# A decoder layer whose feed-forward products are taken by 2x2 blocks with seven multiplications

## The chip, the cores and the metric

The kernel runs on one core of a Trainium2 chip. The metric is the device time of one execution in microseconds (us). The engines are called as in the profile: PE (TensorE, matrix products; PEld is its loading of weights), DVE (VectorE), ACT (ScalarE), POOL (GpSimd) and SP (SyncE), which issues every DMA here.

## The reference

One layer of a hybrid decoder. It takes 1024 prompt tokens and 8 sample tokens (1032 columns in all), 1024 channels, and a feed-forward width of 2816. The part up to the mixing (projections, attention, pooling, gates) is the same in both kernels. The part that is changed computes, per token:

```
m  = sigmoid(gate_a) * (o @ w_attn_o) + sigmoid(gate_b) * B
x  = x + gt1 * (m @ w_out)
h2 = rmsnorm(x) * (1 + sc2) + sh2
gg, up = split(h2 @ w_gu)                    # w_gu: 1024 x (2 x 2816)
y  = x + gt2 * ((silu(gg) * up) @ w_down)    # w_down: 2816 x 1024
```

The sample tokens have shifts, scales and gates of their own; the prompt tokens share one set. All data is float32.

## The kernel before

Activations lie with channels on the 128 partitions and tokens along the free axis, in tiles of 128 channels. A float32 product is made of three matmuls in a 4-byte format of lower precision (`_mm3`, lines 70 to 73): each operand is split into a high part (a rounding copy on ACT, line 97) and a low part (source minus high part, on DVE or POOL, line 106), and high x high, high x low and low x high are summed in PSUM. So every operand costs one pass of ACT and one of DVE or POOL before PE may read it.

Tokens are worked on in three chunks of 344 columns (`C3`). The function `back` (line 1005) begins while attention is still running: it multiplies the attention output of the first six heads by `w_attn_o` for all chunks (tile `pm`, line 1066), then, chunk by chunk, adds the last two heads (`rest`, line 1038), multiplies by `w_out` (line 1099), adds the residual (line 999), forms the mean square with a product by ones (lines 1085, 1086), its root and reciprocal (lines 1113, 1114), and from these h2, split into `h2h` and `h2l`. The 8 weight tiles of `w_out` are split once and stay in SBUF for the three chunks.

`feed_forward` (line 1130) goes through the 22 tiles of the feed-forward width in four parts (`FPARTS`, 6, 6, 5 and 5 tiles). For each tile it loads and splits one weight tile of the gate half and one of the up half (`wload`, 128 x 1024 each), and for each chunk makes the two products over 8 tiles of channels (48 matmuls), then silu on ACT, the product on DVE and a split into `acth` and `actl`, which stay in SBUF. At the end of a part the products with `w_down` for the 8 tiles of output channels are added to x (line 999), which also stays in SBUF. The weights have four pairs of slots, so loading and splitting run ahead of PE.

The order is made by a planner. The program text is traced; the planner then simulates the engines and puts, on each engine, the instruction that is ready and stands first in the text, and sets the semaphores. Two of its rules matter for the steps below. First, tiles with one tag share its slots (`bufs` of them) in the order of the text: the next tile gets a slot when the tile that had it has been read for the last time, even if the data for the next one have long been there. Second, a pool that is opened over the memory or the PSUM banks of a closed pool is not written until everything in the closed pool is done. Each engine then runs its list in order.

## Time and profile before

| | us |
|---|---|
| median of 3 runs (1799.04 to 1801.34) | 1800.38 |
| span of the profiled execution | 1798.7 |
| PE busy | 1741.1 (97%) |
| DVE / ACT / POOL busy | 828.8 / 614.2 / 307.2 |

The own time of the profiled execution outside its span is not given apart; the median of the runs stands 1.7 us above the span, which is taken for what lies around it. PE busy means that a matmul is somewhere in the engine; matmuls overlap, so the distance from one start to the next says how fast PE works, not the duration of one. The stages follow one another: projections and the sample tokens with the gates as filler up to about 600 us, attention of the prompt up to 925 us, `w_out` up to 1047 us, feed-forward up to the end.

### The profile page before, as it was taken

How to read it: one execution, taken by the hardware profiler on the slowest of the kernel's cores; microseconds unless marked ns; L12 is line 12 of the kernel's file. 1: busy time of each engine (PE TensorE's matmuls, PEld its weight loads, DVE VectorE, ACT ScalarE, POOL GpSimd, SP SyncE). 2: the span in 40 equal slices, each digit the busy share in tenths (PEclk: the TensorE clock that was granted, in tenths of full speed). 3: DMA queues.
4: the chain of work that ended last, by engine and by line, in shares of the span. 5: the costliest groups of instructions: out<-in, count | busy, mean ns of one | idle time of the engine just before them, and what ended most of it. 6: DMA issues, size and time to landing. Idle time of an engine off the chain costs nothing.

```text
span 1798.7 us, 30723 instructions
## 1 busy us (share of the span) xinstructions
PE 1741.1 (97%) x11840; PEld 1641.8 (91%) x11840; DVE 828.8 (46%) x1731; ACT 614.2 (34%) x1521; POOL 307.2 (17%) x336
## 2 busy tenths in 40 slices
PE   6799999999999999999989999999999999999999
PEld 5799999789687899998889899999999999999999
DVE  5656665547332455555787852233222322242223
ACT  5433555546341355545542332211221112111210
POOL 2524201001011223222575630000000000000000
PEclk9899999999999999999999999999999999999999
DMA  9213635445636433335523211111111121111112
GB/s 376 63 58 105 209 99 151 147 131 158 186 101 204 157 124 125 124 122 179 158 86 97 70 42 53 36 48 60 47 42 36 53 59 39 30 62 47 39 57 82
DMA packets 112147, 182.70 MB, mean 102 GB/s; under 512 B 15193, under 2 KB 86770, under 8 KB 110978
## 3 DMA queue, kind: packets, MB, share of 16 engines
q1 hardware_dynamic: 112002, 180.75, 32.4%
q8 instruction: 93, 1.52, 0.4%
q14 instruction: 52, 0.43, 0.1%
HBM read 151.77 MB, written 28.93 MB: 100 GB/s over the span
## 4 chain that ended last, share of the span: by engine, by line
PE 80%; DMA 4%; DVE 4%; issue 2%; ACT 1%; POOL 1%; SPq 1%; DVEq 0%; ACTq 0%; POOLq 0%
PE pj L71 19%; PE pj L72 19%; PE pj L73 19%; PE kn L71 4%; PE kn L72 3%; PE kn L73 3%; PE dacc L958 2%; PE tpp L679 2%; PE ada_ps L142 1%; PE av L693 1%; PE av L694 1%; PE sc L71 1%; PE sc L73 1%; PE sc L72 1%; PE tp L628 1%
## 5 line engine op out<-in xcount | busy, mean ns | idle before, releaser
L73 PE MATMUL pj<-h2h,fw 128*128 128x344 f32 x1056 | 337.1, 319 | 0.0
L72 PE MATMUL pj<-h2l,fw 128*128 128x344 f32 x1056 | 336.9, 319 | 0.0
L71 PE MATMUL pj<-h2h,fw 128*128 128x344 f32 x1056 | 335.7, 319 | 0.0
L73 PEld LDWEIGHTS pj<-h2h,fw 128*128 128x128 f32 x1056 | 198.3, 188 | 0.0
L72 PEld LDWEIGHTS pj<-h2l,fw 128*128 128x128 f32 x1056 | 198.2, 188 | 0.0
L71 PEld LDWEIGHTS pj<-h2h,fw 128*128 128x128 f32 x1056 | 198.1, 188 | 0.0
L97 ACT ACTIVATE fw<-fraw 128x1024 fp32r<-128x1024 f32 (+2 forms) x76 | 72.0, 948 | 302.4 <-PE pj L72 302.4
L73 PE MATMUL pj<-acth,fw 128*128 128x344 f32 x528 | 169.0, 320 | 0.0
L72 PE MATMUL pj<-actl,fw 128*128 128x344 f32 x528 | 168.9, 320 | 0.0
L71 PE MATMUL pj<-acth,fw 128*128 128x344 f32 x528 | 168.6, 319 | 0.0
L71 PE MATMUL pj<-hh,wt_hi 128*128 128x344 f32 x480 | 159.8, 333 | 0.0
L1167 DVE TENSOR_TENSOR silu<-silu,pj 128x344 f32<-128x344 f32 x66 | 33.8, 512 | 270.7 <-PE pj L73 270.7
L72 PE MATMUL pj<-hl,wt_hi 128*128 128x344 f32 x480 | 157.5, 328 | 0.0
L73 PE MATMUL pj<-hh,wt_lo 128*128 128x344 f32 x480 | 157.4, 328 | 0.0
L71 PE MATMUL kn<-wuh,lh 128*128 128x256 f32 (+1 forms) x512 | 150.4, 294 | 1.9 <-ACT nr L903 1.0
L72 PE MATMUL kn<-wul,lh 128*128 128x256 f32 (+1 forms) x512 | 145.3, 284 | 0.0
L73 PE MATMUL kn<-wuh,ll 128*128 128x256 f32 (+1 forms) x512 | 144.9, 284 | 0.0
L902 ACT ACTIVATE dsq<-kn 128x256 f32<-128x256 f32 x256 | 95.1, 380 | 111.5 <-PE kn L73 103.5
L999 DVE SCALAR_TENSOR_TENSOR x<-pj,mod,x 128x344 f32<-128x344 f32 (+1 forms) x96 | 55.0, 573 | 149.9 <-PE pj L73 149.9
L106 DVE TENSOR_TENSOR fw<-fraw,fw 128x1024 fp32r<-128x1024 f32 (+2 forms) x76 | 83.5, 1099 | 76.5 <-ACT fw L97 74.5
L904 DVE TENSOR_REDUCE ssq<-dsq 128x8 f32<-128x512 f32 x128 | 86.7, 679 | 52.5 <-ACT dsq L902 52.0
L71 PEld LDWEIGHTS kn<-wuh,lh 128*128 128x128 f32 x512 | 96.6, 189 | 13.0 <-issue 5.7
(328 smaller groups left out, 3778.9 us busy)
## 6 DMA issues: line engine op xcount, KB each, us to landing
fraw<-wgu_t SPq DMA_DIRECT2D x44, 512.0 KB, 3.6
pg<-cpack SPq DMA_DIRECT2D x128, 144.0 KB, 2.4
ln<-cnat SPq DMA_DIRECT2D x128, 128.5 KB, 2.4
wraw<-wada_t SPq DMA_DIRECT2D x32, 512.0 KB, 3.9
wraw<-win_t SPq DMA_DIRECT2D x20, 512.0 KB, 4.2
nat_d<-nat SPq DMA_DIRECT2D x8, 1024.0 KB, 4.5
natr<-nat_d SPq DMA_DIRECT2D x8, 1024.0 KB, 5.2
fraw<-wdn_t SPq DMA_DIRECT2D x16, 384.0 KB, 3.2
```

The source lines that it names most:

```text
L71: nc.tensor.matmul(out, sh, mh, start=first, stop=False)
L72: nc.tensor.matmul(out, sh, ml, start=False, stop=False)
L73: nc.tensor.matmul(out, sl, mh, start=False, stop=last)
L97: nc.scalar.activation(dst, src, AF.Copy)
L106: e.tensor_tensor(dl, src, dh.bitcast(F32), op=ALU.subtract)
L142: nc.tensor.matmul(acc[32 * j:32 * j + 32, 0:P], self.sT[:, kt, :], w[:, kt], start=(kt < 4), stop=(kt >= 4), tile_position=(0, 32 * j))
L679: nc.tensor.transpose(tp[:, s, i * P:(i + 1) * P], pn[:, i, kb * P:(kb + 1) * P], self.ident)
L902: nc.scalar.activation(sq[:, half].rearrange("p h d -> p (h d)"), kn[:, o:o + 256], AF.Square)
L904: nc.vector.tensor_reduce(ssq[:, j, t], sq.rearrange("p a h d -> p (a h) d"), axis=AX.X, op=ALU.add)
L958: nc.tensor.matmul(acc[32 * j:32 * j + 8, :W], p[:, j, t], ln[:, j], start=(t == 0), stop=False, tile_position=(0, 32 * j))
L999: nc.vector.scalar_tensor_tensor(dst[:, s0:], acc[:, s0:], gt[:, j, 8:9], res[:, s0:], op0=ALU.mult, op1=ALU.add)
L1167: nc.vector.tensor_tensor(s, s, accs[1], op=ALU.mult)
```

## The change

Each product of the gate and up halves, and of `w_down`, is made by 2x2 blocks: the weights as [[a11, a12], [a21, a22]], the activations as [[b11, b12], [b21, b22]], and seven products of sums of blocks take the place of eight products of blocks. The left operand's sums (`left`) are made on POOL and split into seven weight tiles `w0` to `w6`; the right operand's (`combine`) are made on DVE and POOL and split into seven pairs of tiles in a pool `M`. In gate and up, the block row is gate / up, the inner index is even / odd channel tile, the block column is the first / second half of the tokens. The halves are cut again in two (`i`), so a matmul has 258 columns (`HC`), and a token half `i` of `back` is the 2 x 258 columns that share one set of sums. The accumulators of PSUM take more than one product: a product is added on top after an engine has read the state before it.

`back` works on two such halves of the tokens in place of three chunks; `w_out` is loaded and split for each half; x after the first residual goes to DRAM (`x1_d`), and so do the activations of the feed-forward (`act_d`). These are read back in three parts of 8, 8 and 6 tiles (`PARTS`, pairs 4, 4 and 3), combined, and multiplied with `w_down`; x is loaded again before that. The tiles of `M` for the sums have the same tags (`c{i}_..`) in gate and up and in the three parts; the scratch tiles of `left` and `combine` share the tags `s0` to `s3` of the pool `sp`.

```diff
-FPARTS = (6, 6, 5, 5)
+PARTS = (4, 4, 3)
+T2 = T // 2
+HC = T // 4
...
     def back(self, c):
...
+        M = c.enter_context(tc.tile_pool(name="M", bufs=1, side="right"))
         W = c.enter_context(tc.tile_pool(name="W", bufs=1))
-        fw = c.enter_context(tc.tile_pool(name="fw", bufs=2))
+        fw = c.enter_context(tc.tile_pool(name="fw", bufs=3))
+        sp = c.enter_context(tc.tile_pool(name="sp", bufs=1))
...
+            pm = r.enter_context(tc.tile_pool(name="pm", bufs=2, space=PSUM))
+            ps = r.enter_context(tc.tile_pool(name="psb", bufs=3, space=PSUM))
+            xo = r.enter_context(tc.tile_pool(name="xo", bufs=1))
+            xw = r.enter_context(tc.tile_pool(name="xw", bufs=2))
...
+            for i in range(2):
+                st = ps.tile([P, 2, 512], F32, name="st2", tag="mm")[:, :, :HC]
+                x1 = [xo.tile([P, T2], F32, name="x1b", tag=f"x{j}") if i else m(f"c1_{16 + j}", "x1a")
+                      for j in range(8)]
...
                 for j in range(8):
+                    raw = fw.tile([P, 8, P], F32, name="fraw")
+                    nc.sync.dma_start(raw, I["wout_t"][j])
+                    wh, wlo = (W.tile([P, 8, P], F32R, name="wout", tag=f"w{3 + 2 * (j % 2) + n}") for n in range(2))
+                    self.split(wh, wlo, raw, "a", WOE[j])
...
+                    for h in range(2):
+                        cs = slice(h * HC, (h + 1) * HC)
+                        for k in range(8):
+                            _mm3(nc, acc[:, h], wh[:, k], wlo[:, k], mh[i][k][:, cs], ml[i][k][:, cs], k == 0, k == 7)
+                    if i == 0:
+                        rest(1, j)
...
+                    nc.sync.dma_start(seg(self.x1_d[j], i), two(x))
+                    sq = xw.tile([P, T2], F32, name="sq2", bufs=1)
+                    nc.scalar.activation(sq, x, AF.Square)
...
+                rs = xw.tile([P, T2], F32, name="rstd2", bufs=1)
+                nc.scalar.activation(two(rs), st, AF.Sqrt, scale=1.0 / DM, bias=self.eps)
                 nc.vector.reciprocal(rs, rs)
                 for j in range(8):
+                    x = x1[j]
+                    nc.vector.tensor_tensor(x, x, rs, op=ALU.mult)
...
+                    nc.scalar.activation(x, x, AF.Identity, scale=self.a2[:, j, 8:9], bias=sh2[:, j, 8:9])
...
+                cm = self.combos(i, 4)
+                for r2 in range(2):
+                    self.combine(cm, r2, [(x1[4 * r2 + 2 * q], x1[4 * r2 + 2 * q + 1]) for q in range(2)])
+                self.comb.append(cm)
+        self.feed_forward(c, gt2)
+    def combos(self, i, n):
+        return [[[self.m(f"c{i}_{14 * r + 2 * o + hl}", "cmb", F32R).rearrange("p (q n) -> p q n", q=2)
+                  for r in range((n + 1) // 2)] for hl in range(2)] for o in range(7)]
+    def combine(self, cm, r, pairs):
+        n = len(pairs)
+        b = [[z[:, 0:HC] for z in p] + [z[:, HC:T2] for z in p] for p in pairs]
+        T1, T2_, T3, T4 = (self.sp.tile([P, T2], F32, name="tcm", tag=f"s{k}").rearrange("p (q n) -> p q n", q=2)
+                           for k in range(4))
+        for q, (b11, b21, b12, b22) in enumerate(b):
+            nc.vector.tensor_tensor(T1[:, q], b12, b11, op=ALU.subtract)
+            nc.gpsimd.tensor_tensor(T3[:, q], b22, b12, op=ALU.subtract)
+            nc.vector.tensor_tensor(T2_[:, q], b22, T1[:, q], op=ALU.subtract)
+            nc.gpsimd.tensor_tensor(T4[:, q], b21, T2_[:, q], op=ALU.subtract)
+        for o, src in enumerate((0, 1, T2_, T3, T1, 3, T4)):
+            hi, lo = (cm[o][hl][r] for hl in range(2))
+            if isinstance(src, int):
+                for q in range(n):
+                    self.split(hi[:, q], lo[:, q], b[q][src], "a")
+            else:
+                self.split(hi[:, :n], lo[:, :n], src[:, :n], "a")
+    def left(self, a11, a12, a21, a22, n):
+        s1, s2, s3, s4 = (self.sp.tile([P, T2], F32, name="scm", tag=f"s{k}")[:, :n * P].rearrange(
+            "p (k m) -> p k m", k=n) for k in range(4))
+        nc.gpsimd.tensor_tensor(s1, a21, a22, op=ALU.add)
+        nc.gpsimd.tensor_tensor(s2, s1, a11, op=ALU.subtract)
+        nc.gpsimd.tensor_tensor(s3, a11, a21, op=ALU.subtract)
+        nc.gpsimd.tensor_tensor(s4, a12, s2, op=ALU.subtract)
+        for o, src in enumerate((a11, a12, s2, s3, s1, s4, a22)):
+            w = self.W.tile([P, 8, P], F32R, name="wst", tag=f"w{o}")
+            self.split(w[:, 0:n], w[:, 4:4 + n], src, "a")
...
+    def feed_forward(self, c, gt2):
+        ps = c.enter_context(tc.tile_pool(name="psf", bufs=8, space=PSUM))
+        with tc.tile_pool(name="ffe", bufs=2) as ev:
+            for f in range(NF):
...
+                w = self.left(raws[0][:, 0::2], raws[0][:, 1::2], raws[1][:, 0::2], raws[1][:, 1::2], 4)
+                run = lambda acc, o, i, more=False: self.product(acc, o, w, self.comb[i], 4, more)
+                for i in range(2):
+                    b[i] = bank("fb")
+                    run(b[i], 0, i)
+                    p1[i] = t("p1")
+                    nc.scalar.activation(p1[i], b[i], AF.Copy)
...
+                for i in range(2):
+                    run(b[i], 4, i, True)
+                    u4[i] = t("u4")
+                    nc.scalar.activation(u4[i], b[i], AF.Copy)
...
+                for i in range(2):
+                    run(b[i], 5, i, True)
...
+                for i in range(2):
+                    run(d[i], 6, i, True)
+                    nc.vector.tensor_tensor(u2[i], d[i], u2[i], op=ALU.add)
+                    nc.gpsimd.tensor_tensor(act[i][:, :HC], c11[i], u2[i], op=ALU.mult)
+                    nc.sync.dma_start(self.seg(self.act_d[f], i), act[i].rearrange("p (h n) -> p h n", h=2))
+        xp = c.enter_context(tc.tile_pool(name="xp2", bufs=1))
+        for j in (0, 4, 1, 5, 2, 6, 3, 7):
+            x = xp.tile([P, T], F32, name="xacc", tag=f"xa{j}")
+            nc.sync.dma_start(x, self.x1_d[j])
...
+        for part, n in enumerate(PARTS):
+            cms = [self.combos(i, n) for i in range(2)]
+            for r in range((n + 1) // 2):
+                for i in range(2):
+                    pairs = []
+                    for q in range(2 * r, min(n, 2 * r + 2)):
+                        z = xp.tile([P, 2, T2], F32, name="actr")
+                        for k in range(2):
+                            nc.sync.dma_start(z[:, k].rearrange("p (h n) -> p h n", h=2),
+                                              self.seg(self.act_d[f0 + 2 * q + k], i))
+                        pairs.append((z[:, 0], z[:, 1]))
+                    self.combine(cms[i], r, pairs)
+            for j in range(4):
...
+                w = self.left(raws[0][:, 0::2], raws[0][:, 1::2], raws[1][:, 0::2], raws[1][:, 1::2], n)
+                run = lambda acc, o, i, more=False: self.product(acc, o, w, cms[i], n, more)
...
+                for i in range(2):
+                    run(b[i], 4, i, True)
+                    add(j + 4, i, 1, b[i])
...
+                for i in range(2):
+                    run(b[i], 5, i, True)
+                    add(j, i, 1, b[i])
...
+            f0 += 2 * n
```

`product` makes 3 matmuls for each of its `n` pairs of tiles; `add` is one `scalar_tensor_tensor` of DVE that adds gate times accumulator to the x tile.

## Rows read from the trace of the kernel before

**Rows 1.** The page: span, and busy time, share and instructions of each engine.
```profile
span 1798.7 us, 30723 instructions
PE 1741.1 (97%) x11840; PEld 1641.8 (91%) x11840; DVE 828.8 (46%) x1731; ACT 614.2 (34%) x1521; POOL 307.2 (17%) x336
```

**Rows 2.** The page's chain of waits, shares of the span by engine.
```profile
PE 80%; DMA 4%; DVE 4%; issue 2%; ACT 1%; POOL 1%; SPq 1%; DVEq 0%; ACTq 0%; POOLq 0%
```

**Rows 3.** Windows: stretch, length, busy (xinstructions), clock, DMA share, GB/s.
```profile
core 0: us, PE busy (x) PEld busy (x) DVE busy (x) ACT busy (x) POOL busy (x), PEclk, DMA share, GB/s
10.00:20.00 10.00, 3.98 (x30) 3.56 (x30) 6.20 (x6) 6.37 (x7) 1.29 (x1) 1.00 1.03 414
925.00:935.00 10.00, 7.92 (x35) 7.06 (x36) 10.00 (x13) 5.57 (x9) 8.12 (x7) 0.83 0.32 80
1047.00:1795.00 748.00, 748.00 (x4760) 747.90 (x4758) 217.30 (x382) 134.74 (x217) 7.91 (x9) 1.00 0.16 48
```

**Rows 4.** Groups by line and form, PE: count, then busy us and mean ns.
```profile
L71 PE MATMUL pj<-h2h,fw 128*128 128x344 f32 x1056 | 335.7, 319 | 0.0
...
L71 PE MATMUL pj<-acth,fw 128*128 128x344 f32 x528 | 168.6, 319 | 0.0
```

**Rows 5.** Timeline of PE near 303 us: start, duration, operation, columns.
```profile
302.02 0.28 PE L71 MATMUL kn<-wuh,lh 128*128 128x256 f32 x1
...
302.73 0.32 PE L73 MATMUL pj<-hh,wt_lo 128*128 128x344 f32 x1
...
303.37 0.28 PE L71 MATMUL kn<-wuh,lh 128*128 128x264 f32 x1
...
304.11 0.32 PE L71 MATMUL pj<-hh,wt_hi 128*128 128x344 f32 x1
```

**Rows 6.** Groups by line and form, DVE, from 880 us on.
```profile
L106 DVE TENSOR_TENSOR actl<-silu,acth 128x344 fp32r<-128x344 f32 x66 | 33.9, 514 | 23.5 <-ACT acth L97 23.5
...
L106 DVE TENSOR_TENSOR ml<-mt,mh 128x344 fp32r<-128x344 f32 x24 | 22.8, 967 | 0.5 <-ACT mh L97 0.5
...
L106 DVE TENSOR_TENSOR fw<-fraw,fw 128x640 fp32r<-128x640 f32 x16 | 13.2, 826 | 11.4 <-ACT fw L97 10.9
...
L1114 DVE RECIPROCAL rstd<-rstd 128x344 f32<-128x344 f32 x3 | 6.9, 2303 | 8.1 <-ACT rstd L1113 8.1
```

**Rows 7.** Groups by line and form, ACT, from 880 us on.
```profile
L97 ACT ACTIVATE acth<-silu 128x344 fp32r<-128x344 f32 x66 | 32.2, 488 | 165.2 <-DVE silu L1167 165.1
...
L97 ACT ACTIVATE fw<-fraw 128x640 fp32r<-128x640 f32 x16 | 11.8, 740 | 70.5 <-PE pj L72 70.5
```

**Rows 8.** Groups by line and form, POOL, whole span.
```profile
L1104 POOL TENSOR_TENSOR sq<-x 128x344 f32<-128x344 f32 x24 | 20.5, 856 | 39.8 <-DVE x L999 21.0 <-DVE x L1003 11.9 <-ACT fw L97 6.7
...
L106 POOL TENSOR_TENSOR v<-natr,v 128x512 fp32r<-128x512 f32 x8 | 10.3, 1281 | 32.9 <-ACT v L97 32.9
```

**Rows 9.** The page's DMA issues: count, KB each, us from issue to landing.
```profile
fraw<-wgu_t SPq DMA_DIRECT2D x44, 512.0 KB, 3.6
...
sa<-sga_d SPq DMA_DIRECT2D x24, 172.0 KB, 3.6
...
xr<-xT SPq DMA_DIRECT2D x24, 172.0 KB, 2.3
o_yT<-x SPq DMA_DIRECT2D x24, 172.0 KB, 1.8
```

**Rows 10.** Timeline of DVE at the end of w_out: start, duration, operation.
```profile
1047.57 0.58 DVE L999 SCALAR_TENSOR_TENSOR x<-pj,mod,xr 128x344 f32<-128x344 f32 x1 [1.52 <-PE pj L73]
1049.61 0.52 DVE L106 TENSOR_TENSOR sql<-sq,sqh 128x344 fp32r<-128x344 f32 x1 [1.46 <-ACT sqh L97]
1054.29 2.30 DVE L1114 RECIPROCAL rstd<-rstd 128x344 f32<-128x344 f32 x1 [4.16 <-ACT rstd L1113]
```

**Rows 11.** Timeline of ACT where attention ends: idle and releaser in brackets.
```profile
926.75 2.01 ACT L97 ACTIVATE wout<-fraw 128x1024 fp32r<-128x1024 f32 x2 [1.07 <-DMA o_d<-ot]
```

More of the change, by code (lines that the diff above doesn't have):

```diff
@@ L993, in decode_out @@
         nc.sync.dma_start(self.o_d[:, :, 0:NB].rearrange("a p c -> p a c"), os)
-    def gated_add(self, dst, acc, gt, j, res, i, pool):
-        nc = self.nc
-        s0 = NB if i == 0 else 0
-        nc.vector.scalar_tensor_tensor(dst[:, s0:], acc[:, s0:], gt[:, j, 8:9], res[:, s0:], op0=ALU.mult, op1=ALU.add)
-        if s0:
-            t = pool.tile([P, NB], F32, name="gas")
-            nc.vector.tensor_tensor(t, acc[:, :NB], gt[:, j, 0:8], op=ALU.mult)
-            nc.vector.tensor_tensor(dst[:, :NB], t, res[:, :NB], op=ALU.add)
@@ new lines, in back @@
+        fw = c.enter_context(tc.tile_pool(name="fw", bufs=3))
+        sp = c.enter_context(tc.tile_pool(name="sp", bufs=1))
+        self.M, self.W, self.fw, self.sp = M, W, fw, sp
+        self.x1_d = self.dram.tile([8, P, T], F32, name="x1_d")
+        self.act_d = self.dram.tile([NF, P, T], F32, name="act_d")
+        m = lambda tag, name, dt=F32: M.tile([P, T2], dt, name=name, tag=tag)
+        self.m = m
+        seg = lambda ap, i: ap.rearrange("p (h n) -> p h n", h=2)[:, :, i * HC:(i + 1) * HC]
@@ L1076, in back @@
                 rest(0, j)
-            wo, x1 = [], []
-            for i in range(NCH):
-                cs = slice(i * C3, (i + 1) * C3)
-                st = ps.tile([P, 512], F32, name="st2", tag="mm")[:, :C3]
-                x1.append(xo.tile([P, 8, C3], F32, name=f"x1_{i}", tag=f"x{i}"))
+            self.comb = []
+            for i in range(2):
+                st = ps.tile([P, 2, 512], F32, name="st2", tag="mm")[:, :, :HC]
+                x1 = [xo.tile([P, T2], F32, name="x1b", tag=f"x{j}") if i else m(f"c1_{16 + j}", "x1a")
+                      for j in range(8)]
@@ L1082, in back @@
                 sqs = []
                 def stat(j):
-                    nc.tensor.matmul(st, onesr, sqs[j][0], start=(j == 0), stop=False)
-                    nc.tensor.matmul(st, onesr, sqs[j][1], start=False, stop=(j == 7))
+                    for h in range(2):
+                        for n in range(2):
+                            nc.tensor.matmul(st[:, h], onesr, sqs[j][n][:, h * HC:(h + 1) * HC],
+                                             start=(j == 0 and n == 0), stop=(j == 7 and n == 1))
@@ L1092, in back @@
-                        a, b = (slot(2 * j + n, f"wout{n}")[:, :DM].rearrange("p (k m) -> p k m", k=8) for n in range(2))
-                        self.split(a, b, raw, "a", WOE[j])
-                        wo.append((a, b))
-                    xr = xw.tile([P, C3], F32, name="xr")
-                    nc.sync.dma_start(xr, I["xT"][j][:, cs])
-                    acc = ps.tile([P, 512], F32, name="pj", tag="mm")[:, :C3]
-                    for k in range(8):
-                        _mm3(nc, acc, wo[j][0][:, k], wo[j][1][:, k], mh[i][k], ml[i][k], k == 0, k == 7)
@@ L1100, in back @@
[L1100 to L1106 removed]
+                        gates_in(1, j)
+                    xr = xw.tile([P, T2], F32, name="xr")
@@ new lines, in back @@
+                    nc.sync.dma_start(two(xr), seg(I["xT"][j], i))
+                    acc = ps.tile([P, 2, 512], F32, name="pj", tag="mm")[:, :, :HC]
+                    for h in range(2):
+                        cs = slice(h * HC, (h + 1) * HC)
+                        for k in range(8):
[3 more added lines that the diff above has]
+                    x = x1[j]
@@ new lines, in back @@
+                    nc.vector.scalar_tensor_tensor(two(x), acc, gt1[:, j, 8:9], two(xr), op0=ALU.mult, op1=ALU.add)
+                    if i == 0:
+                        t = xw.tile([P, NB], F32, name="gas")
+                        nc.vector.tensor_tensor(t, acc[:, 0, :NB], gt1[:, j, 0:8], op=ALU.mult)
+                        nc.vector.tensor_tensor(x[:, :NB], t, xr[:, :NB], op=ALU.add)
+                    nc.sync.dma_start(seg(self.x1_d[j], i), two(x))
+                    sq = xw.tile([P, T2], F32, name="sq2", bufs=1)
@@ L1107, in back @@
+                    nc.scalar.activation(sq, x, AF.Square)
+                    sqh = xw.tile([P, T2], F32R, name="sqh")
+                    sql = xw.tile([P, T2], F32R, name="sql")
                     self.split(sqh, sql, sq, "a")
@@ new lines, in product @@
+    def product(self, acc, o, w, cm, n, more=False):
+        nc = self.nc
+        kw = dict(skip_group_check=True) if more else {}
+        for q in range(n):
+            (sh, sl), mh, ml = w[o], cm[o][0][q // 2][:, q % 2], cm[o][1][q // 2][:, q % 2]
+            nc.tensor.matmul(acc, sh[:, q], mh, start=(q == 0 and not more), stop=False, **kw)
+            nc.tensor.matmul(acc, sh[:, q], ml, start=False, stop=False, **kw)
+            nc.tensor.matmul(acc, sl[:, q], mh, start=False, stop=(q == n - 1), **kw)
```

260 lines of the change are left out of this document (137 added, 123 removed).

## The prediction

> **What bounds the kernel now.** I read four views. First the page's busy times: PE is busy for 97% of the span, every other engine under half [rows 1]. Then the chain of waits: 80% of it is PE [rows 2], so the end moves with PE's work as long as PE is fed. Then the windows: from 1047 to 1795 us, the feed-forward, PE runs 4760 matmuls in 748 us without a gap at the full clock while DVE has 217 us and ACT 135 us of work, so PE alone bounds this stage; earlier, from 925 to 935 us, PE gets 35 matmuls done at a granted clock of 0.83, DVE is busy throughout and POOL for 8 us of 10 [rows 3]. Last the price of a matmul. The duration of 319 ns [rows 4] is not it, since matmuls overlap: 748 us / 4760 = 157 ns from start to start with 344 columns. For 258 columns the nearest rows are those of the sample tokens: six of 256 columns take 302.73 - 302.02 = 0.71 us, six of 264 take 304.11 - 303.37 = 0.74 us [rows 5], 118 and 123 ns; I take 119.
>
> **The change part by part.** *Matmuls.* Before, gate, up and down take (1056 + 528) x 3 = 4752 matmuls [rows 4]: 4752 x 157.1 = 747 us. After, a column of gate and up (one tile of the width) is 7 products x 4 pairs x 3 x 2 halves = 168 matmuls, 22 of them 3696; down is 4 columns x 7 x 3 x 2 x (4 + 4 + 3) = 1848. 5544 x 0.119 = 660 us. Gain 87 us. (With 118 or 123 ns: 93 or 65.) In `back`, `w_out` goes from 576 x 157.1 to 768 x 119 (+1 us), the other products likewise (+1): 2 us.
>
> *Work that feeds PE inside a stage.* A column lasts 168 x 0.119 = 20 us. POOL makes four sums of 128x512 at 1.28 us [rows 8] and four products of about 0.65: 8 us. ACT splits seven tiles and copies five accumulators per half, DVE the low parts and three sums per half: under 8 us each from 514 ns for 344 and 826 for 640 columns, ACT 488 and 740 [rows 6, 7], from which I work out 0.42 us for 258 and 0.69 for 516 on DVE, 0.38 and 0.62 on ACT. All this lies beside PE, since a weight tile is free as soon as its product is done, a column ahead. Tight is one place: product 5 is added onto a bank that ACT (gate, up) or DVE (down) must have read after product 4, and only the other half's product, 1.43 us, lies between. I take 5 us over all 34 columns (0 to 15).
>
> *Start of w_out.* Two halves in place of three chunks, on an already starved stretch [rows 3]; fewer gate loads crowd the time before. I take 0 (-5 to +10).
>
> *End of w_out to the first column.* Now a chunk's root and norm hide behind other chunks. With two halves the second has nothing behind it: PSUM of the new pool waits for the old pools (the root must have read `st2`), and the evacuation tiles `ffe` wait until all of `xo` and `xw` has been read, that is until the second half is combined. That the planner waits for whole pools shows in the row of `wout`, released by the last DMA out of attention's pool [rows 11]. From the last matmul: residual sum, square, copy, low part, 4 products, root, by 344-column rows [rows 6, 7, 10] scaled to 516 about 4.7 us; reciprocal 2.30 x 516/344 = 3.5; eight products on DVE 8 x 0.69 = 5.5; then combine. One combine of two pairs costs DVE 4 x 0.42 for T1, T2, 6 x 0.42 and 4 x 0.69 for low parts: 7.0 us, two of them 14. Sum 27.7. The scratch of `left` comes after that of `combine` in the text and shares its tags, so the sums for product 2 start only then: two POOL sums and an ACT copy, 2 x 1.28 + 0.6, less some 1.4 by which their slots are free earlier: 29.5 us. Meanwhile PE has products 0 and 1 of both halves, 4 x 1.43 = 5.7 us. Loss 24 us (15 if half of the combine slips ahead, 36 if DVE runs at the 967 ns of `ml` in place of 514 [rows 6]).
>
> *Boundaries of the parts of down.* The sums of a new part use the same tags of `M` as the last; a tile is free only when the last column has used its product. And the activations come back through one slot, `actr` (its pool has one buffer): a pair is loaded, read by T1 to T4 and three direct splits, and only then the next load starts. Price of such a turn: two DMAs of 258 KB each, between the 1.8 us of a 172 KB store and the 3.6 us of 172 KB gate loads in a crowd or of 512 KB of weights, I take 3.0 until DVE can start (nearest to the uncrowded 2.3) [rows 9]; then DVE 5 x 0.42 = 2.1 for the first pair of a combine, and 2.1 + 3 x 0.69 = 4.2 for the second, whose sixth split stands behind three of T. So a combine takes u = 3.0 + 2.1 + 3.0 + 4.2 = 12.3 us (7.8 with 1.8 us loads and only direct work, 19.1 with 3.6 us loads and DVE at the contended price).
> Part 1 to part 2 (four combines): the first pair is loaded early but needs product 5 of the last column, 4.3 us before the end E; it is gone at E - 3.4; its partner is read at E - 3.4 + 7.2 = 3.8; three more combines, 3 x 12.3; then 2.0 for `left`'s sums, which wait for the last T; less the 5.7 us of products that PE has meanwhile: 3.8 + 36.9 + 2.0 - 5.7 = 37 us (20 to 62).
> Part 2 to part 3 (the second two combines have one pair, 6.4 us): 3.8 + 12.3 + 12.8 + 1.7 - 4.3 = 26 us (14 to 45).
> Gate and up to part 1: the pool `xp2` lies over `ffe`, so even the first loads wait for the last store of the activations: 0.4 + 0.65 + store about 2.5 = 3.6 us. Ahead of the first pair SP issues the eight loads of x, 4.2 MB; at 414 GB/s [rows 3] 10.3 us. First pair there at 3.6 + 1.9 + 10.3 + 1.3 = 17.1; 17.1 + 2.1 + 7.2 + 36.9 + 2.0 - 5.7 = 60 us (35 if its loads pass those of x, 86).
>
> *Clock.* After a wait PE is granted less: 0.83 over ten us after a starved stretch [rows 3], 1.7 us. Four stretches: 7 us (3 to 10).
>
> *Sum.* -87 + 2 + 5 + 0 + 24 + 60 + 37 + 26 + 7 = +74 us on a span of 1798.7, and 1.7 us outside it as before: 1874 us, my forecast. With every bound at its low end the sum is -9, at its high end +201.
>
> The Trainium skill, "SBUF — State Buffer", section "Who interferes with whom", says that a DVE instruction with two SBUF inputs and a GpSimd instruction that reads SBUF take the same read interface, and that one blocks the other for its whole length. By it T1, T2 and the low parts would run one after another with T3 and T4, which is the case of the third rival; the `ml` rows agree (967 ns beside a busy POOL, 514 without).
>
> **The rivals.** *One: the boundaries are hidden, the kernel is faster.* If the loads ran ahead and the tiles came free one product after another, PE would go on with product 0 while the rest is made, and a boundary would cost about 5 us, the end of `w_out` 14: -87 + 2 + 14 + 15 + 7 + 5 = -44, 1756 us. For it: the tiles do come free in the order in which the next column needs them. Against: one slot for the pairs and the scratch order of the text. It decides by u: the three boundaries are 9u + 12, and the other terms are -49, so the sum is zero at u = 4.1 us, when the two loads of a turn alone take 3.6 at the least. Chance 0.17.
> *Two: it cancels.* With u = 7.8, the early combine and the other terms as taken the sum is -87 + 2 + 5 + 15 + 35 + 20 + 14 + 3 = +7, and a term a little lower makes it zero: 1800 us. For it: each low end is a row; against: all would have to hold together. Chance 0.05.
> *Three: DVE and POOL hold each other up.* u = 19.1 and combine at the contended price: 86 + 62 + 45 + 36 in place of 147, +156, 1956 us. For it: the rows of `ml`; against: at a boundary little else runs, and the load is half of a turn. Chance 0.06.
> That matmuls of 258 columns gain nothing is excluded by rows 5.
>
> **How the numbers follow.** My forecast has 0.72, its own range is 1825 to 1920. Range for 8 in 10: 1780 to 1920; below lie the better half of rival one, above rival three. A measurement tells 0.2% (3.6 us) from no change. Faster 0.17, same 0.05, slower 0.78.
>
> **What would show it.** Right: PE gaps of some 20 us or more at four places (after the last `wout` matmul, after column 22, after the fourth and eighth column of down), the one after gate and up the longest; `actr` loads one by one with DVE and ACT work between them; inside a column no gaps, and matmuls 119 ns apart. Wrong: PE starts product 2 of a part within 10 us of the end of the last; or PE gaps in every column, which would move the loss from the boundaries into the stage; or 258 columns at much over 120 ns.

## The result and the profile after

The changed kernel takes 1903.91 us (median of 4 runs, 1902.95 to 1904.70), the kernel before beside it 1800.86 us: a ratio of 1.0575 (95% interval 1.056 to 1.059). The prediction was 1874 us and slower; the direction and the places came out as it said, and 30 us of size were missing. The profiled execution has a span of 1902.0 us, 103.3 more than before.

The page: span and busy times, and of the chain of waits the shares by engine. Against [rows 1, 2]:

```profile
span 1902.0 us, 34644 instructions
PE 1710.7 (90%) x12936; PEld 1596.7 (84%) x12936; DVE 1056.4 (56%) x2122; ACT 793.8 (42%) x1950; POOL 552.1 (29%) x545
...
PE 71%; DVE 8%; DMA 8%; issue 2%; ACT 1%; POOL 1%; SPq 1%; DVEq 0%; ACTq 0%; POOLq 0%
```

PE's share falls from 97% to 90% and on the chain from 80% to 71%; what takes its place is DVE and DMA (4% each before). Windows of five stretches (columns as in [rows 3]): after `w_out`; the steady part of gate and up; after gate and up; between parts 1 and 2 of down; between parts 2 and 3:

```profile
1058.75:1087.35 28.60, 12.91 (x56) 10.27 (x54) 24.25 (x39) 17.61 (x34) 12.77 (x9) 0.70 0.03 10
1100.00:1500.00 400.00, 400.00 (x3323) 400.00 (x3323) 162.56 (x261) 155.64 (x340) 169.87 (x161) 1.00 0.28 81
1530.40:1602.24 71.84, 18.49 (x53) 12.90 (x53) 39.69 (x67) 21.47 (x46) 20.87 (x22) 0.53 0.39 132
1678.70:1728.46 49.76, 17.41 (x54) 12.17 (x52) 35.87 (x61) 20.29 (x43) 18.46 (x18) 0.56 0.27 81
1804.90:1840.42 35.52, 12.69 (x43) 9.11 (x42) 27.67 (x53) 15.85 (x37) 12.94 (x14) 0.58 0.25 74
```

In the second row PE starts 3323 matmuls in 400 us: 120.4 ns each, without a gap. With that price the loss of a stretch is its length less its matmuls: 28.60 - 56 x 0.1204 = 21.9 us after `w_out`, then 65.5, 43.3 and 30.3 us. The losses below are counted so. They leave out the matmuls that still run at the lower clock behind a window, which cost another 1.6 to 2.1 us at each boundary here; counted up to where PE is back at 0.12 us a matmul, the three boundaries lose 67.0, 45.0 and 32.4 us. PE's own waits from 1087 us on (line, what ended them: us in total, times, longest):

```profile
PE fb L1193 <- ACT cmb L97: 84.8, 20, 18.1
PE fa L1194 <- DVE cmb L106: 12.0, 13, 1.4
PE fb L1193 <- ACT wst L97: 11.3, 4, 3.6
PE fd L1193 <- ACT wst L97: 7.4, 3, 6.5
```

Twenty waits for a high part of `combine` make up 85 us; the longest, 18.1 us, is the first after gate and up. The chain of waits there shows what each of them is made of (start, us, what):

```profile
1534.94 4.39 DMA xacc<-x_d
1539.35 8.76 DMA actr<-act_d
1548.12 0.43 ACT cmb L97
...
1551.15 2.95 DMA actr<-act_d
1554.12 0.43 DVE tcm L1159
1554.57 0.34 DVE cmb L106
...
1554.95 0.43 DVE tcm L1161
1555.38 2.28 DVE cmb L106 x3
...
1557.72 2.97 DMA actr<-act_d
1560.78 0.43 DVE tcm L1159
```

Each load starts when DVE has read the pair before it, and DVE starts when the load has landed: about 3 us of load and 3 us of DVE in turn. The groups of DVE from 1530 to 1603 us say the same from DVE's side (the last column is idle time and what ended it):

```profile
L106 DVE TENSOR_TENSOR cmb<-actr,cmb 128x258 fp32r<-128x258 f32 x24 | 15.8, 677 | 0.4 <-ACT cmb L97 0.3
L106 DVE TENSOR_TENSOR cmb<-tcm,cmb 128x516 fp32r<-128x516 f32 x16 | 13.7, 888 | 0.0
L1161 DVE TENSOR_TENSOR tcm<-actr,tcm 128x258 f32<-128x258 f32 x8 | 4.0, 494 | 0.4 <-DMA actr<-act_d 0.2
L1159 DVE TENSOR_TENSOR tcm<-actr 128x258 f32<-128x258 f32 x8 | 3.4, 428 | 28.7 <-DMA actr<-act_d 28.7
```

T1 (line 1159) stands for 28.7 us of waiting for loads; the work itself is 37 us for four combines, where the low parts take 677 and 888 ns against the 420 and 690 that were taken for them. One low part while POOL is idle, and one while POOL makes T4:

```profile
1593.07 0.43 DVE L106 TENSOR_TENSOR cmb<-actr,cmb 128x258 fp32r<-128x258 f32 x1
1595.23 0.86 DVE L106 TENSOR_TENSOR cmb<-actr,cmb 128x258 fp32r<-128x258 f32 x1
```

```profile
1594.71 1.10 POOL L1162 TENSOR_TENSOR tcm<-actr,tcm 128x258 f32<-128x258 f32 x1
```

Of the 24 low parts of 258 columns the six with POOL idle take 0.41 to 0.43 us, the eighteen beside it 0.76 on average.

Last, where attention ends and `w_out` ends (lines of tiles: min/median/max ns, first and last start); before, then after:

```profile
L694 PE MATMUL av<-pTl,v x160: 221/282/387, 608.7 to 922.6; 128*128 128x256 f32 x128, 128*128 128x128 f32 x32
L73 PE MATMUL pj<-mh,wout x192: 313/319/492, 931.1 to 1047.2; 128*128 128x344 f32 x192
```

```profile
L694 PE MATMUL av<-pTl,v x160: 220/281/415, 610.9 to 919.7; 128*128 128x256 f32 x128, 128*128 128x128 f32 x32
L73 PE MATMUL pj<-mh,wout x256: 277/282/583, 936.9 to 1058.4; 128*128 128x258 f32 x128
```

From the last matmul of attention to the last of `w_out` it is 124.6 us before and 138.7 after. Attention ends some us earlier or later from one execution to the next, so this length, and not the end of `w_out`, is compared below.

### The profile page after: what moved, and what is told of

The parts are those of the page before. It is cut to its first block, busy times and chain, and to the rows that moved or that the text cites. A ratio compares the mean times of both kernels' runs of the same rounds, so it can differ in the third digit from the quotient of the medians.

```text
span 1902.0 us, 34644 instructions
## 1 busy us (share of the span) xinstructions
PE 1710.7 (90%) x12936; PEld 1596.7 (84%) x12936; DVE 1056.4 (56%) x2122; ACT 793.8 (42%) x1950; POOL 552.1 (29%) x545
## 4 chain that ended last, share of the span: by engine, by line
PE 71%; DVE 8%; DMA 8%; issue 2%; ACT 1%; POOL 1%; SPq 1%; DVEq 0%; ACTq 0%; POOLq 0%
PE fb L1195 6%; PE fb L1193 6%; PE fb L1194 6%; PE pj L71 5%; PE pj L72 5%; PE pj L73 5%; DMA actr<-act_d 4%; PE kn L71 3%; PE fd L1193 3%; PE fd L1194 3%; PE fd L1195 3%; PE kn L72 3%; PE kn L73 3%; DVE cmb L106 3%; PE dacc L958 2%
## 5 line engine op out<-in xcount | busy, mean ns | idle before, releaser
L1193 PE MATMUL fb<-cmb,wst 128*128 128x258 f32 x1056 | 309.7, 293 | 100.1 <-ACT cmb L97 87.9
L1194 PE MATMUL fb<-cmb,wst 128*128 128x258 f32 x1056 | 308.7, 292 | 3.1 <-DVE cmb L106 3.1
L1195 PE MATMUL fb<-cmb,wst 128*128 128x258 f32 x1056 | 303.3, 288 | 0.3 <-DVE wst L106 0.3
L1193 PEld LDWEIGHTS fb<-cmb,wst 128*128 128x128 f32 x1056 | 205.8, 195 | 107.4 <-ACT cmb L97 94.0
L1194 PEld LDWEIGHTS fb<-cmb,wst 128*128 128x128 f32 x1056 | 206.0, 195 | 7.0 <-DVE cmb L106 7.0
L1195 PEld LDWEIGHTS fb<-cmb,wst 128*128 128x128 f32 x1056 | 206.0, 195 | 0.5 <-DVE wst L106 0.5
L106 DVE TENSOR_TENSOR wst<-scm,wst 128x512 fp32r<-128x512 f32 (+1 forms) x136 | 109.0, 809 | 173.8 <-ACT wst L97 171.3
L1193 PE MATMUL fd<-cmb,wst 128*128 128x258 f32 x528 | 151.4, 287 | 7.5 <-ACT wst L97 7.4
L1194 PE MATMUL fd<-cmb,wst 128*128 128x258 f32 x528 | 150.3, 285 | 0.0
L1195 PE MATMUL fd<-cmb,wst 128*128 128x258 f32 x528 | 148.2, 282 | 0.0
L97 ACT ACTIVATE wst<-scm 128x512 fp32r<-128x512 f32 (+1 forms) x136 | 83.5, 615 | 148.7 <-PE fb L1195 64.4
L1193 PEld LDWEIGHTS fd<-cmb,wst 128*128 128x128 f32 x528 | 100.5, 190 | 8.7 <-ACT wst L97 8.7
L1178 POOL TENSOR_TENSOR scm<-fraw 128x512 f32<-128x512 f32 (+1 forms) x34 | 45.4, 1337 | 214.0 <-DVE wst L106 188.7
```

Of the source, the lines that this page charges most:

```text
L97: nc.scalar.activation(dst, src, AF.Copy)
L106: e.tensor_tensor(dl, src, dh.bitcast(F32), op=ALU.subtract)
L1178: nc.gpsimd.tensor_tensor(s3, a11, a21, op=ALU.subtract)
L1193: nc.tensor.matmul(acc, sh[:, q], mh, start=(q == 0 and not more), stop=False, **kw)
L1194: nc.tensor.matmul(acc, sh[:, q], ml, start=False, stop=False, **kw)
L1195: nc.tensor.matmul(acc, sl[:, q], mh, start=False, stop=(q == n - 1), **kw)
```

## The experiments

Theory S says that the one slot for pairs, with its load and work in turn, makes the boundaries; rival D, that DVE with POOL beside it, or tiles of `M` that come free late, would hold PE up just as long. A second question came with the profile: why `w_out` takes 14 us more.

**Two slots for the pairs**

```diff
-                        z = xp.tile([P, 2, T2], F32, name="actr")
+                        z = xp.tile([P, 2, T2], F32, name="actr", bufs=2)
```

> The changed kernel with two buffers for the pairs of activations (actr), nothing else. Changed kernel: 1903.9 us; time that PE loses beyond 0.12 us per matmul: 65.5 us after gate and up, 43.3 between parts 1 and 2, 29.7 between parts 2 and 3. Theory S (one slot makes load and DVE work follow one another, about 3.05 + 2.95 us a pair): the next load now runs beside the work on a pair, a turn falls from 6.0 to about 3.5 us (DVE's work with POOL beside it); 7 turns after gate and up, 7 and 5 later, and one more pair is there before the last column ends: -18, -20, -14, sum about -50, 1854 us (1840 to 1870). Rival D (DVE and POOL, or tiles of M that come free late, set the pace and the loads only fill the wait): 1885 to 1904 us.

1846.29 us (1843.22 to 1847.37), 1.0254 of before (1.0237 to 1.0271). One buffer more gives back 58 us; S expected 50 and D at most 19. Windows of the three boundaries:

```profile
1530.00:1588.33 58.33, 23.97 (x87) 18.35 (x85) 41.45 (x71) 22.78 (x47) 22.88 (x23) 0.56 0.54 181
1662.44:1684.85 22.41, 11.24 (x32) 7.76 (x32) 22.41 (x43) 13.62 (x28) 11.92 (x12) 0.53 0.41 118
1768.55:1782.46 13.91, 5.91 (x19) 3.93 (x17) 13.91 (x31) 8.26 (x19) 4.50 (x6) 0.53 0.27 77
```

Losses 47.9, 18.6 and 11.6 us. Counted up to where PE is back at full speed they are 47.9, 23.4 and 16.9, so that the three boundaries give back 56 us, the whole gain of the profiled span. In the second and third row DVE is busy for the whole stretch: with the loads out of the way DVE is late next.

**One load for all sums**

```diff
-                        z = xp.tile([P, 2, T2], F32, name="actr")
-                        for k in range(2):
+                        if part == 0 and r == 0 and i == 0 and q == 0:
+                            z0 = xp.tile([P, 2, T2], F32, name="actr")
+                        z = z0
+                        for k in range(2 if part == 0 and r == 0 and i == 0 and q == 0 else 0):
```

> The changed kernel with one pair of activations loaded once; all sums of all parts are made from that one tile, so 42 of 44 loads are left out and the sums have the wrong data; every sum, split and product is still made. It prices what DVE, ACT and POOL need at a boundary without loads. Theory S: the boundaries fall by 3.05 us a pair, 7, 8 and 6 of them: 65.5 to 44, 43.3 to 19, 29.7 to 12 us; span about 1838 us. Rival D: the boundaries stay within 15 us in all, span 1887 or more.

1825.87 us (one run), span 1824.1: 78 us less than the changed kernel, more than S expected (64). The three windows:

```profile
1530.64:1581.76 51.12, 10.79 (x52) 9.01 (x50) 34.79 (x66) 18.48 (x43) 19.13 (x18) 0.59 0.27 104
1665.39:1674.30 8.91, 0.28 (x3) 0.07 (x1) 8.91 (x17) 3.05 (x5) 3.92 (x4) 0.75 0.00 1
1757.15:1762.05 4.90, 0.29 (x4) 0.08 (x2) 4.90 (x12) 1.89 (x4) 1.92 (x2) 0.99 0.01 2
```

Losses 44.9, 8.5 and 4.4 us. Of the second boundary's 43.3 us, 35 go with the loads, since without them DVE does most of its work while the last column still runs. The first stays at 45, and PE's two long waits there say why:

```profile
PE fb L1193 <- ACT cmb L97: 18.2, 1, 18.2
PE fd L1193 <- ACT wst L97: 17.8, 1, 17.8
```

The first pair still comes late, and then PE waits for a weight of `left`, whose scratch comes free only as the fourth combine is done with it, with DVE busy all the while. What is left at the second boundary is the same wait (8.6 us). A scratch of its own for `left` at these boundaries was not tried. Even without these loads the kernel is slower than before.

**The loads of x behind part 1**

```diff
-        for j in (0, 4, 1, 5, 2, 6, 3, 7):
-            x = xp.tile([P, T], F32, name="xacc", tag=f"xa{j}")
-            nc.sync.dma_start(x, self.x1_d[j])
...
                     self.combine(cms[i], r, pairs)
+            if part == 0:
+                for j in (0, 4, 1, 5, 2, 6, 3, 7):
+                    x = xp.tile([P, T], F32, name="xacc", tag=f"xa{j}")
+                    nc.sync.dma_start(x, self.x1_d[j])
```

> The changed kernel with the eight loads of x for w_down after the pairs of part 1 in the text instead of ahead of them. In the changed kernel the first pair is there 17.6 us after the last gate and up matmul, of which 13.2 us pass while loads of x and the pair share the queues. If these stand ahead of everything, as the prediction had it: -8 us, 1896 (1893 to 1899). Rival: with one slot the second pair's load waits for DVE, the loads of x go out in between and hold up the second pair instead of the first: within 3 us, 1901 to 1906.

1900.85 us (1899.22 to 1902.10), 3 us less: the rival, and not the 8 us. PE has its first pair after 8 us in place of 18, and then waits 11 for the second. The traffic of x costs the same wherever it falls between two pairs of one slot.

**Slots that are there before gate and up end** (this and the loads of x later)

```diff
+        ar = c.enter_context(tc.tile_pool(name="ar", bufs=2))
         with tc.tile_pool(name="ffe", bufs=2) as ev:
...
-                        z = xp.tile([P, 2, T2], F32, name="actr")
+                        z = ar.tile([P, 2, T2], F32, name="actr")
```

> Two slots for pairs as in e1, but in a pool of their own that is opened ahead of the evacuation tiles of gate and up, so the first pairs can be loaded while gate and up still run; the loads of x stand behind the pairs of part 1. In e1 PE loses 48.2 us after gate and up, 18.6 and 11.9 us at the other two boundaries. If the difference of 30 us is the wait for the memory of the closed pool and the loads that start only then, this boundary falls to that of parts 1 and 2: about 19 us, 1846 - 29 = 1817 us (1810 to 1828). Rival (x, read back only then, or the last columns' stores hold up the adds and with them DVE): 1835 us or more.

1834.05 us (1829.24 to 1838.61), 1.0182 of before (1.0154 to 1.0211): between the two. Window of the first boundary, and two pieces of the chain inside it:

```profile
1532.00:1566.86 34.86, 13.37 (x51) 9.22 (x49) 29.28 (x53) 16.04 (x35) 16.56 (x18) 0.58 0.70 245
```

```profile
1540.85 5.44 DMA xacc<-x_d
...
1546.66 9.38 DMA actr<-act_d
```

The loss is 28.7 us, against 47.9 with the two late slots: 19 of the 29 us expected. Behind this window PE still runs at the lower clock; windows over the whole of each boundary show what remains:

```profile
1520.00:1600.00 80.00, 58.28 (x403) 53.92 (x403) 57.85 (x101) 28.29 (x57) 33.55 (x30) 0.79 0.44 146
1630.00:1700.00 70.00, 56.61 (x391) 52.24 (x390) 57.14 (x106) 27.12 (x53) 28.58 (x24) 0.83 0.34 99
1735.00:1805.00 70.00, 58.26 (x436) 55.72 (x435) 56.22 (x129) 24.14 (x53) 25.67 (x24) 0.88 0.31 93
```

By these the first boundary loses 31.5 us in place of 47.9, so 16 us are gained. Two things were changed, the pool and the place of the loads of x, and they were not tried apart here (the loads of x alone gained 3 us). Part of the rest is x again: one pair takes 9.4 us to land behind the eight loads of x, and PE waits 9.4 us there. The three boundaries together still lose 72 us with two early slots, half of the changed kernel's 144.

**Plain down**

```diff
+        ar = c.enter_context(tc.tile_pool(name="ar", bufs=2))
         with tc.tile_pool(name="ffe", bufs=2) as ev:
...
+        ring = [(o, r) for o in range(7) for r in range(2)]
+        for part, n in enumerate(DPARTS):                        # 8, 7, 7 tiles
+            act = []
+            for k in range(f0, f0 + n):
+                o, r = ring[k % 14]
+                z = ar.tile([P, T], F32, name="actr")
+                nc.sync.dma_start(z, self.act_d[k])
+                act.append([[self.m(f"c{h}_{14 * r + 2 * o + hl}", "act2", F32R) for hl in range(2)] for h in range(2)])
+                for h in range(2):
+                    self.split(*act[-1][h], z[:, h * T2:(h + 1) * T2], "a")
...
+            for js in (((0, 1), (2,), (3,), (4,), (5,), (6,), (7,)) if part == 0 else [(j,) for j in range(8)]):
...
+                order = [(a, k) for k in range(n) for a in accs] if len(js) > 1 else [(a, k) for a in accs for k in range(n)]
```

> Gate and up as in the changed kernel; w_down with plain products (2112 matmuls of 258 columns instead of 1848), its activations still through DRAM, in three parts of 8, 7 and 7 tiles that lie in M as plain high and low parts, with two slots for loading that are there while gate and up still run; the first output tiles of part 1 take the activations tile by tile as they come. If the loss is one of the one slot and of sums that all have to be there before a product: three boundaries of 138.5 us fall to about 8 in all, 264 more matmuls cost 31.7 us, the clock stays up (-4): 1801 us (1790 to 1815). Rival (the way through DRAM itself, load and split of every activation, costs what the boundaries cost): 20 us or more stay at each, 1850 us or more.

1790.78 us (1788.54 to 1792.75), 0.9955 of before (0.9939 to 0.9972): 113 us less than the changed kernel and 0.4% less than the kernel before. Window of all of down, from 2 us ahead of the end of gate and up:

```profile
1528.00:1783.00 255.00, 255.00 (x2126) 254.98 (x2124) 96.41 (x194) 40.25 (x56) 3.89 (x4) 1.00 0.32 105
```

PE has no gap at any of the three boundaries, at the full clock. The activations go through DRAM, are split and share memory with the sums of gate and up as in the changed kernel; the rival is refuted. What is gone is that a product needs sums over the pairs of a whole part, and that these come through one slot. With the sums went all that belongs to them (T1 to T4, POOL's work beside DVE, the sums of `left` and their scratch), and two early slots and products that take tile by tile came at the same time; which of these counts for how much of the last 72 us was not tried apart.

**The text order in back**, alone and with plain down (the lines of the norm products and combine are moved as they are)

```diff
                 nc.vector.reciprocal(rs, rs)
-                for j in range(8):
+                late.append((x1, rs))
+            for i, (x1, rs) in enumerate(late):                  # after both halves' loops of w_out
+                if i:
+                    self.w0 = self.wcol(0)                       # left of column 0
+                for j in range(8):
                     x = x1[j]
```

> The changed kernel with another order of the text in back alone: norm products and combine of the first half stand after the loop of w_out of the second half (so they fill DVE's idle time instead of going first), and left of column 0 stands ahead of the second combine. In the changed kernel w_out ends at 1058.7 us, 11.5 later than before; between 1018 and 1043 PE waits 2.2 and 3.9 us for DVE and then works some 40 matmuls at half clock, and after w_out PE loses 22.1 us. Theory F (the first half's combine, 14 us of DVE, stands ahead of the second half's residuals and squares; and left's scratch waits for the second combine): w_out ends 6 to 9 us earlier and the loss after it falls by about 4 us (products 0 to 6 of the first half, 10 us, in place of products 0 and 1 of both, 5.7): 1892 us (1888 to 1896). Rival (DVE's work is the bound of this stretch, so what is put off is paid after w_out): w_out ends earlier but the loss after it grows as much: 1900 to 1908.

> Plain w_down (as in e5) and the order of e4 together. If the two don't touch: 1790.8 us less what e4 gains, about 1779 us (1775 to 1784) by theory F, 1787 to 1795 by the rival.

1902.02 us (1899.81 to 1904.62) and 1788.72 us (1784.79 to 1790.73): 2 us less each, within the spread of the runs, so theory F is wrong and the rival's times came out. The loss after `w_out` falls as expected (window 1060.82 to 1088.51: 83 matmuls in 27.69 us, 17.7 us), but from the end of attention to the last `w_out` matmul it is 139.5 us, no shorter. So this order of DVE's work is not what makes `w_out` long.

**The first half's sums left out**

```diff
+                if i == 0:
+                    continue
                 cm = self.combos(i, 4)
...
-                self.comb.append(cm)
+                self.comb += [cm, cm]
```

> The changed kernel without combine of the first half; gate and up use the second half's sums for both halves (wrong data, all their matmuls are made). It prices those sums in the stretch of w_out, where PE loses 8.7 us between 1015 and 1047 us (4.4 before the change) and w_out ends at 1058.7. If they (16.8 us of DVE there) are what holds PE up: w_out ends 5 to 8 us earlier, at 1051 to 1054. Rival (DVE is late there for other reasons: norm products and instructions of 8 columns that take up to 2.3 us beside POOL): within 2 us of 1058.7.

1900.64 us (one run); from attention to the end of `w_out` 136.0 us. This stretch is 138.4 to 140.4 us long in the profiles of the changed kernel and of the five versions above that leave it as it is, so the sums hold `w_out` up for 2.4 to 4.4 us, less than the 5 to 8 expected.

**POOL idle in w_out** (with plain down)

```diff
-WOE = 'pvppvppv'
+WOE = 'vvvvvvvv'
...
-                nc.gpsimd.tensor_tensor(t, gb[i][j], t, op=ALU.add)
+                nc.vector.tensor_tensor(t, gb[i][j], t, op=ALU.add)
```

> e5 with the low parts of w_out and the gated sum of rest all on DVE instead of POOL, so POOL has next to nothing to do between 925 and 1010 us. In the changed kernel, 900 to 1060 us, DVE's ml of 516 columns takes 1.18 us where sql without POOL takes 0.69, x1a by rstd 1.17 against 0.75 for x1b, the instructions of 8 columns 0.15 to 2.3: about 26 us that DVE loses beside POOL, and the moved work is 10 x 1.21 + 16 x 0.70 = 23 us. Theory L (an instruction of DVE with two inputs waits for POOL's to end): ml falls to 0.7 us, and w_out ends within 4 us of e5's 1057.5: 1787 to 1795 us. Rival (the long durations come from the DMA traffic there): ml stays over 1 us and w_out ends 10 us or more later: 1800 or more.

1783.93 us (1781.18 to 1786.92), 0.9897 of before (0.9879 to 0.9915); with POOL it was 0.9955 (0.9939 to 0.9972). The group of `ml` in the changed kernel, and its tile's line here:

```profile
L106 DVE TENSOR_TENSOR ml<-mt,mh 128x516 fp32r<-128x516 f32 x16 | 18.9, 1183 | 5.8 <-ACT mh L97 5.4
```

```profile
L106 DVE TENSOR_TENSOR ml<-mt,mh x16: 683/692/697, 935.2 to 1009.1; 128x516 fp32r<-128x516 f32 x16
...
L694 PE MATMUL av<-pTl,v x160: 221/281/472, 611.2 to 923.9; 128*128 128x256 f32 x128, 128*128 128x128 f32 x32
...
L73 PE MATMUL pj<-mh,wout x256: 277/282/419, 939.5 to 1056.1; 128*128 128x258 f32 x128
```

All sixteen `ml` take 0.69 us, none over 0.70, in place of 1.18 on average: theory L, and the time is 3 us below its range. DVE is given 26 instructions more and still `w_out` is 132.2 us long, 7 less than with plain down alone (139.4). So DVE's waits for POOL cost 7 us of this stretch. It does not follow that they are half of the 14 us that the change added, as the windows from attention's end to the end of `w_out` show, before, in the changed kernel and here:

```profile
922.60:1047.20 124.60, 114.50 (x680) 109.86 (x681) 99.29 (x167) 44.47 (x79) 76.73 (x67) 0.97 0.29 85
919.70:1058.40 138.70, 122.98 (x939) 118.88 (x939) 111.71 (x174) 64.38 (x101) 54.24 (x34) 0.94 0.52 156
923.90:1056.10 132.20, 120.68 (x941) 116.26 (x940) 107.79 (x200) 64.25 (x101) 7.13 (x8) 0.97 0.55 166
```

POOL has 77 us of work there before the change and 54 after it: its low parts of `w_out` double (13 to 26 us), but the squares and the scaling of h2 (39 us before) have gone to ACT. In the kernel before, `ml` takes 967 ns beside POOL [rows 6] too. What a POOL at rest would give there was not tried. By PE's count, 680 matmuls at 0.157 us leave a loss of 17.8 us before, 939 at 0.1204 one of 25.6 after, and 18.9 with POOL idle: of the 14 us some 6 are matmuls and 8 are loss.

**POOL's two sums of combine on DVE, and left ahead of the second combine** (one on top of the other)

```diff
-            nc.gpsimd.tensor_tensor(T3[:, q], b22, b12, op=ALU.subtract)
+            nc.vector.tensor_tensor(T3[:, q], b22, b12, op=ALU.subtract)
...
-            nc.gpsimd.tensor_tensor(T4[:, q], b21, T2_[:, q], op=ALU.subtract)
+            nc.vector.tensor_tensor(T4[:, q], b21, T2_[:, q], op=ALU.subtract)
```

```diff
+                if i:
+                    self.w0 = self.wcol(0)
                 cm = self.combos(i, 4)
```

> e8 with the two sums of combine that POOL makes (T3, T4) on DVE too. After w_out PE loses 22 us in the changed kernel; its chain there goes through POOL's T4 and T3 (2.24 us for one instruction that takes 0.65 alone, 4.05 us without a recorded reason, then 2.0 us), while DVE works beside it. Theory L: without POOL that piece of 8.3 us becomes DVE work of 4 x 0.42 us for the four T3, T4 of a combine, two combines 3.4 us: the loss falls by about 5 us, 1783.9 to about 1779 us (1776 to 1782). Rival (DVE is the bound after w_out, POOL only fills): 3.4 us more on DVE, 1784 to 1789.

> e12 with left of column 0 ahead of the second combine in the text, as in e4 (there the loss after w_out fell from 22.1 to 18.1 us, but with the first half's sums put off as well w_out ended 1.5 us later). Theory: another 3 to 4 us, about 1776 us (1772 to 1780). Rival (the seven splits of left, 4.8 us of DVE, then fall into w_out, where DVE is full): within 2 us of e12.

The first alone: 1786.70 us (1784.53 to 1789.35), 0.9921 (0.9904 to 0.9938), no gain that can be told from the one without it. The loss after `w_out` is 24.4 us, and one wait in it explains why nothing came of it:

```profile
PE fd L1193 <- ACT wst L97: 8.6, 1, 8.6
```

The rival's time came out. The last of the sums is ready 1.8 us earlier behind the end of `w_out` than with POOL, but the sums of `left`, which stay on POOL and whose scratch comes after theirs in the text, start hardly earlier, and the first takes 3.4 us beside the busy DVE, where none took over 1.73 in the version before:

```profile
1078.56 3.40 POOL scm L1176
```

With `left` moved: 1776.43 us (1773.85 to 1777.80), 0.9866 of before (0.985 to 0.9883), the fastest version here. That wait is gone, as the windows after `w_out` and of the steady parts of gate and up and of down show:

```profile
1050.95:1076.88 25.93, 16.56 (x80) 14.05 (x78) 24.07 (x46) 17.01 (x33) 1.59 (x1) 0.74 0.17 51
1090.00:1510.00 420.00, 420.00 (x3489) 420.00 (x3488) 171.22 (x276) 165.57 (x358) 173.71 (x164) 1.00 0.29 86
1516.50:1768.00 251.50, 251.50 (x2098) 251.50 (x2097) 95.49 (x193) 38.54 (x53) 3.22 (x3) 1.00 0.33 103
```

16.3 us are lost after `w_out`. The gain of 10 us is more than twice what was expected of the move; in the kernel without it the wait had grown from 6.4 to 8.6 us. `left` moved alone, with POOL's two sums left in `combine`, was not tried with plain down.

## Why the prediction was right, and where its sizes were off

By its own terms, in us of the profiled span:

| term | predicted | measured |
|---|---|---|
| matmuls of gate, up, down | -87 | -79 |
| up to the end of `w_out` (start, and its matmuls) | +2 | +11 (14 longer, attention ended 3 earlier) |
| end of `w_out` to the first column | +24 | +22 |
| gate and up to part 1 | +60 | +65.5 |
| part 1 to 2 | +37 | +43 |
| part 2 to 3 | +26 | +30 |
| inner stalls and clock | +12 | +10 (what is left) |
| sum | +74 | +103 |

The range held the result and every row has the sign that was forecast; the sum was 29 us short. Of these 16 are the boundaries, 9 the stretch up to the end of `w_out` and 8 the matmuls; the other two rows were 4 us too high.

*Matmuls.* 5544 x 0.1204 = 667.5 us against 4752 x 0.1571 = 746.5. The spacing was taken from six matmuls in a row [rows 5] as 119 ns and is 120.4, inside the 118 to 123 that the rows gave. That 1.4 ns is 8 us: over thousands of instructions the spacing has to come from a long stretch.

*The boundaries* are where the prediction put them, in its order, with the gap after gate and up the longest, and by its mechanism, which two slots and no loads showed from both sides. The first pair is there 17.9 us after the last gate and up matmul (1548.1 less the last start at 1530.2), predicted 17.1. A combine was to cost u = 12.3 us. Measured from the first pair at 1548.1 to the last low part at 1598.1, with the first load: (50.0 + 3.05) / 4 = 13.3. The loads were right (3.0 us), DVE was not: its low parts take 677 and 888 ns where 420 and 690 were taken, because POOL's T3, T4 and `left` run beside them. The three boundaries make 22 pairs, 11 combines' worth, so at 1 us each (as measured at the first) that is 11 us; `left`'s sums at the end took 1.6 + 1.7 + 0.6 = 4 us at the first two in place of 2, another 4. Together 15 of the 16 us that the boundaries are longer than predicted. (Rival one's sum has 9u + 12 for the three boundaries; by their own terms u counts about 11 times, 11u - 13, and the whole sum is zero at u = 5.6 us and not 4.1, which is still far below 13.3.)

*Start of w_out, taken as 0 (-5 to +10).* This stretch is 14 us longer by the length from attention's end, of which 2 had been priced as matmuls of `back`. Measured are 6 us of matmuls (940 at 0.1204 against 680 at 0.157; 116 in place of 60 are for `w_attn_o`, 20 of them of the first six heads, which before were done by then) and 8 us of loss, inside the range given but not at its middle. The prediction saw that the stretch was starved and DVE busy in it [rows 3], but priced only what halves in place of chunks do to the loads. What it left out: with two halves the first half's sums of gate and up fall on a DVE that was already busy for 99 of 125 us, which leaving them out put at 2.4 to 4.4 us. Taking POOL out gives back 7, but POOL is less busy there than before the change, so no run shows how much of the 8 us comes from it. One candidate for the rest, not tried, is that the first six heads' product is now gated only in `rest`, which adds two DVE instructions per tile at the very start.

*Rival three* had a mechanism that is there, at a much smaller price. The Trainium skill, "SBUF — State Buffer", section "Who interferes with whom", has a DVE instruction with two SBUF inputs and a GpSimd instruction that reads SBUF exclude each other. The runs agree: `ml` falls from 1.18 to 0.69 us when POOL is idle. At the boundaries, where the prediction looked for it, it costs about 1 us a combine, some 11 us, where this rival had added 70, slower loads included; in `w_out`, where POOL's longest instructions take 2.6 us, taking POOL out gives 7. *Rival one* (hidden boundaries) is refuted for this kernel, but plain down, where they are hidden, has what it asked for: a store that is there before the last stage ends, two slots, and products that take each tile as it comes.

*Clock.* The granted clock is 0.53 to 0.58 in the three boundaries, and the first matmuls behind each run at the lower of the two levels (1.2 GHz), some 0.21 us apart at a granted clock of 0.51 from 1602 to 1606 us, before they return to 0.12. Behind the four windows that costs 3.5, 1.6, 1.7 and 2.1 us, 9 in all (1.4 of it one more wait after `w_out`), for the 7 predicted. Inside the columns, where 5 us had been set aside, PE loses under 1 us.

The 79 us of fewer multiplications are real, and 53 of them are gate and up's (3168 x 0.1571 - 3696 x 0.1204 = 53). Down's share, 249 - 222.5 = 26 us, can't pay for three boundaries of 139 us together, nor for the 72 that are left with two early slots. The seven products in gate and up alone, with plain down and with what is lost around `w_out` cut from 36 us (14 and 21.9) to 22 (5.6 and 16.3), are worth 1.3%.

## What to carry to other kernels

A form that saves multiplications replaces independent products by sums over whole stages: count first what PE can do while a new stage's sums are made, for each stage, and set that against the matmuls saved. One buffer between a load and its reader costs the sum of both at every turn, and a pool over a closed pool's memory starts that only when the old stage is over: a second slot was worth 58 us here and the earlier pool (with x moved) 12, while the orders of the text that were tried gave 2 to 10. Where DVE is the late engine, work moved to POOL is not free: look for DVE durations that vary where the shape doesn't.

## What the runs showed that was not expected

- DVE got 26 more instructions of 0.7 to 1.2 us and the stage became 7 us shorter, since POOL hardly ran beside it any more (7 us of work in place of 54). Instructions of 8 columns, 0.15 us alone, had taken up to 2.3 us next to POOL's.
- Eight loads of x (4.2 MB) lengthen one load of a pair from 3.0 to 8.8 to 9.4 us in all three places that were tried with `combine` in down; moving them behind the first pair gained 3 us where 8 were expected.
- Taking POOL out of `combine` alone gained nothing, and with `left` moved the two gave some 6 us together (0.9897 to 0.9866 of before): the wait for `left` had grown by about what the sums had gained.
